# Scoring attention B in pairs of heads, and moving attention A's transposes between two projections

## The chip, the core and the metric

The kernel runs on one core of a Trainium2 chip. A core has a matrix engine (TensorE, "PE" in the profile, with its weight loads shown apart as "PEld"), a vector engine (VectorE, "DVE"), a scalar engine (ScalarE, "ACT"), GpSimd ("POOL") and SyncE ("SP"), which issues most transfers. Matrix results land in PSUM and are copied from there to SBUF by DVE or ACT. The metric is the device time of one execution in microseconds (us), of which the median of several runs is taken.

## The reference

One layer of a streaming encoder, batch 1, 256 frames of width 2048, all in float32. The change touches only the middle block, which mixes two attentions:

```python
def hybrid_mixer(u, w_in, ...):
    proj = u @ w_in
    qa, ka, va, q_lat, kv_lat, gates = jnp.split(proj, list(IN_SPLITS), axis=-1)
    y_a = chunked_relbias_attention(qa, ka, va, rel_bias) @ w_o_a   # 16 heads of 64
    y_b = mla_attention(q_lat, kv_lat, ...) @ w_o_b                 # 16 heads of 128 + 64
    g_a, g_b = jnp.split(sigmoid(gates + gate_bias), 2, axis=-1)
    return (g_a * y_a + g_b * y_b) @ w_out
```

Attention A: scores of one head are `q k^T / 8 + bias`, with q and k 64 wide. Attention B: q and k of a head consist of 128 "nope" columns of its own and 64 rotary columns; the rotary key is shared by all heads. Its scores are therefore a sum of two products, `(q_nope k_nope^T + q_rope k_rope^T) / sqrt(192)`. In both, 256 queries look at keys in chunks of 64, causally by chunk, so that the first 128 queries need 128 keys and the second 128 need 256. Then softmax, and the product with v.

Around it stand two feed-forward blocks, a cross attention to 256 memory rows, and layer norms; they are most of the work and are not touched.

## The kernel before, in words

**Precision.** Large products are made from split operands: each weight and each activation is held as hi + lo, and three products (hi hi, hi lo, lo hi) are summed. ACT makes hi (L211), DVE makes lo (L214) from the raw weights, which SP loads two items ahead. The products inside the two attentions (scores, transposes, PV) use plain f32 operands; the profile shows each such matmul as two passes, and a transpose as one.

**The list of items.** `mixer` appends items to `self.items`: a function and the weights that it needs. `run` goes through the list in order and issues the instructions. The framework's planner then fixes, at build time, the order on each engine: earlier items come first, shifted by `prio` (`NEAR` for a softmax), but where an instruction's operands aren't ready by the planner's own estimate, it takes other work that is. So the order in the trace can differ from the list.

**Attention A** works on 8 pairs of heads. `a_proj(i)` makes q and k of pair i, 128 rows for two heads of 64 (`mm_wide`, L263 and L264, two weights, each with 32 matmuls). `a_scores(i)` makes the scores of the two heads: head 0 has its q and k on rows 0 to 63 of the array, head 1 on rows 64 to 127 (L824, "64*128" in the profile). DVE adds the bias (L840; POOL loads it per head) and the softmax follows on DVE and ACT (L695 to L702). `a_trans(i)` transposes the probabilities on TensorE (L707, three 128x128 blocks a head), ACT copies them to SBUF (L713), and `a_out(i)` multiplies with v (`pv`, L854 and L855; "128*64", since a head's v has 64 columns, and the two heads lie on two column halves). Before the change, round i runs: both projections of pair i + 1, transposes of pair i - 1, scores of pair i, PV of pair i - 1.

**Attention B** works on 16 heads, one at a time. `b_proj(h)` makes q and k (24 matmuls, L252; every fourth head also v for four heads, L283). `b_scores(h)` makes, for each of two query blocks `(c0, tt, nk)` of `CAUSAL`, the 128-row product of the nope part and right behind it the 64-row product of the rotary part, into one PSUM tile:

```python
for c0, tt, nk in spans_q:
    for j, (q, k) in enumerate(parts):          # parts: (nope q, k), (rotary q, k)
        nc.tensor.matmul(ps[:, c0:c0 + nk], q[:, tt * P:(tt + 1) * P], k[:, :nk], ...)   # L824
```

The rotary queries of heads 2p and 2p + 1 lie in `self.rt[:, p, :]` on rows 0 to 63 and 64 to 127, and `self.krope` holds the rotary key on both halves. DVE adds the mask (L935), softmax, transposes (L707), copy (L713), PV (L854, L855 with 128 columns) and a split of the result into hi and lo (L242, L243). Round h runs: scores(h), transposes(h - 1), projection(h + 2), PV(h - 1).

**Buffers** that the order hangs on: four PSUM banks for scores, transposes and PV (`at_tile`), four for projections (`mm_tile`); six `w1` tiles (256 wide: q and k) and five `w2` tiles (512 wide: bias, scores, transposed probabilities).

Of the kernel before, what the change touches and what calls it, by code (L numbers as in the profile page):

```python
# [13 lines left out]
ALU = mybir.AluOpType  # L14
# [3 lines left out]
P = 128  # L18
# [9 lines left out]
A_HEADS, A_DIM = 16, 64  # L28
B_HEADS, NOPE, ROPE, V_DIM = 16, 128, 64, 128
# [9 lines left out]
SOON, NEAR, LATE = 400, 100, -400  # L39
# [44 lines left out]
class Kernel:  # L84
# [632 lines left out]
    def mixer(self, xT, st, steps):  # L717
        nc, t = self.nc, self.t
        SPANS = ((0, P), (P, 3 * P))
# [23 lines left out]
        ps = {}  # L743
# [3 lines left out]
        a, b, c = steps(1)  # L747
# [16 lines left out]
        def rms(which):  # L764
            def fn():
                if which == 0:
                    self.sq = self.block("X3")
                    self.c = self.act(["X0", "X1"])
                l = self.lat[:, 4 * which:4 * which + 4, :]
                sq = self.sq[:, 4 * which:4 * which + 4, :]  # L770
                nc.scalar.activation(sq, l, AF.Square)
                ps = self.at_tile()
                for j in range(4):
                    nc.tensor.matmul(ps[:, :S], self.ones, sq[:, j, :], start=(j == 0), stop=(j == 3))
                v, y, a = self.w1(), self.w1(), self.w1()
                nc.vector.tensor_scalar(v, ps[:, :S], 1.0 / LORA, RMS_EPS, ALU.mult, ALU.add)
                self.rsqrt(v, y, a)
                for j in range(4):
                    nc.vector.scalar_tensor_tensor(
                        l[:, j, :], l[:, j, :], self.vec(("q_a_norm", "kv_a_norm")[which], j), y,  # L780
                        ALU.mult, ALU.mult)
                self.split(l, self.c.blk(0, 4 * which, 4), self.c.blk(1, 4 * which, 4))
            self.add(fn)
# [25 lines left out]
        def a_proj(i):  # L809
            def one(k):  # L810
                def fn(w):
                    ps = self.mm_tile()
                    self.mm_wide(ps, w, xT())
                    qk[i, k] = self.total(ps)
                return fn
            for k in range(2):
                self.add(one(k), t["w_qk"][i, k])

        def scores(parts, spans_q):

            ps = self.at_tile()
            for c0, tt, nk in spans_q:
                for j, (q, k) in enumerate(parts):
                    nc.tensor.matmul(ps[:, c0:c0 + nk], q[:, tt * P:(tt + 1) * P], k[:, :nk],  # L824
                                     start=(j == 0), stop=(j == len(parts) - 1))
            return ps

        CAUSAL = ((0, 0, P), (P, 1, S))

        def a_scores(i):  # L830
            def fn():
                for j in range(2):
                    bias = self.w2((P, 3 * P))
                    nc.gpsimd.dma_start(bias, t["bias"][2 * i + j])
                    self.mask_out(bias)
                    rows = slice(64 * j, 64 * j + 64)
                    ps = scores([(qk[i, 0][rows], qk[i, 1][rows])], CAUSAL)
                    s = self.w2()
                    with self.prio(NEAR):
                        nc.vector.scalar_tensor_tensor(s[:, :3 * P], ps[:, :3 * P], 1.0 / math.sqrt(A_DIM), bias,  # L840
                                                       ALU.mult, ALU.add)
                        self.softmax(s, SPANS)
                    sc[i, j] = s
            self.add(fn)

        def a_trans(i):
            def fn():
                for j in range(2):
                    pt[i, j] = self.transpose_p(sc.pop((i, j)), (0, P, 2 * P))
            self.add(fn)  # L850

        def pv(ps, v, pT):

            nc.tensor.matmul(ps[:, :S], v(0), pT[:, :S], start=True, stop=False)  # L854
            nc.tensor.matmul(ps[:, P:S], v(1), pT[:, S:S + P], start=False, stop=True)  # L855

        def a_out(i):
            def fn():
                if i == 0:
                    oA["t"] = self.act(["H4", "H5"])  # L860
                ps = self.at_tile()
                for j in range(2):
                    c = (2 * i + j) * A_DIM
                    pv(ps[64 * j:64 * j + 64], lambda kt: va["t"][:, kt, c:c + A_DIM], pt.pop((i, j)))
                self.split(ps[:, :S], oA["t"].at(0, i), oA["t"].at(1, i))
            self.add(fn)


        rope_items = []
# [16 lines left out]
                nc.vector.tensor_tensor(self.rt[:, j, :], self.rt[:, j, :], sw[:, j, :], ALU.add)  # L886
        rope_items.append((rope_q, (), 0, LATE))

        rms(0)
        a_proj(0)  # L890
        rms(1)
        NA = A_HEADS // 2
        for i in range(NA + 1):
            if i + 1 < NA:
                a_proj(i + 1)
            if i == 1:
                self.items += rope_items
            if i > 0:
                a_trans(i - 1)
            if i < NA:  # L900
                a_scores(i)
            if i > 0:
                a_out(i - 1)

        bq, bsc, bpt, bv, oB = {}, {}, {}, {}, {}

        def b_proj(h):
            def vfn(w, g=h // 4):
                if g == 0:
                    bv["t"] = self.block("X3", (P, 2, 2, 512))  # L910
                for tt in range(2):
                    ps = self.mm_tile()
                    self.mm_tok(ps, tt, w, self.c, range(4, 8), True, True)
                    (nc.scalar.copy if tt else nc.vector.tensor_copy)(bv["t"][:, g % 2, tt, :], ps)
            if h % 4 == 0:
                self.add(vfn, t["w_v"][h // 4])

            def fn(w):
                for k in range(2):
                    ps = self.mm_tile()  # L920
                    self.mm_feat(ps[:, :S], w, [(0, k * 512 + j * P) for j in range(4)], self.c,
                                 range(4 * k, 4 * k + 4))
                    v = self.w1()
                    (nc.scalar.copy if k == 0 else nc.vector.tensor_copy)(v, ps[:, :S])
                    bq[h, k] = v
            self.add(fn, t["w_nope"][h])

        def b_scores(h):
            def fn():
                rows = slice(64 * (h % 2), 64 * (h % 2) + 64)  # L930
                ps = scores([(bq.pop((h, 0)), bq.pop((h, 1))),
                             (self.rt[rows, h // 2, :], self.krope[rows])], CAUSAL)
                s = self.w2()
                with self.prio(NEAR):
                    nc.vector.scalar_tensor_tensor(s[:, :3 * P], ps[:, :3 * P], float((NOPE + ROPE) ** -0.5),  # L935
                                                   self.mask, ALU.mult, ALU.add)
                    self.softmax(s, SPANS)
                bsc[h] = s
            self.add(fn)

        def b_trans(h):
            def fn():
                bpt[h] = self.transpose_p(bsc.pop(h), (0, P, 2 * P))
            self.add(fn)

        def b_out(h):
            def fn():
                if h == 0:
                    oB["t"] = self.act(["H0", "H1", "H2", "H3"])
                ps = self.at_tile()  # L950
                pv(ps, lambda kt: bv["t"][:, h // 4 % 2, kt, h % 4 * P:h % 4 * P + P], bpt.pop(h))
                self.split(ps[:, :S], oB["t"].at(0, h), oB["t"].at(1, h))
            self.add(fn)

        b_proj(0)
        b_proj(1)
        for h in range(B_HEADS + 1):
            if h < B_HEADS:
                b_scores(h)
            if h > 0:  # L960
                b_trans(h - 1)
            if h + 2 < B_HEADS:
                b_proj(h + 2)
            if h > 0:
                b_out(h - 1)


        mix, gt = {}, {}
# [317 lines left out]
```

## Time and profile before

| | before |
|---|---|
| time, median of 3 runs | 2561.37 us (2556.62 to 2562.75) |
| span of the profiled execution | 2560.8 us (the page gives no other time for it) |
| TensorE busy | 2544.3 us, 99% |
| TensorE weight loads busy | 2144.3 us, 84% |
| DVE busy | 1734.4 us, 68% |
| ACT busy | 1247.1 us, 49% |
| granted TensorE clock | 0.998 |
| DMA | 189 GB/s over the span |
| mixer's attentions, 832.9 to 1060.0 us | 227.1 us, TensorE busy 226.13 |

A row of the timeline gives the start in us, the length in us, the engine, the line of the kernel, the operation, the output and input tiles, the shape and how many instructions are merged; in brackets stands idle time of the engine before it and who ended it. For a matmul the shape begins with the part of the array that is used ("64*128": 64 rows, 128 columns), then the operand moved through it. "at" is a tile of the four banks for scores, transposes and PV, "mm" one of the projections' banks. A row of the windows gives, for a stretch of time, the busy us of each engine with its instruction count, the granted clock, the DMA share and GB/s.

### The profile page before, as it was taken

The numbers are of one execution on the slowest core, as the hardware profiler recorded it, in microseconds if no ns is written. First come the engines' busy times: TensorE is split into PE (matmuls) and PEld (weight loads), VectorE is DVE, ScalarE is ACT, GpSimd is POOL, SyncE is SP. The second block draws the span as 40 slices with busy tenths as digits, with TensorE's granted clock in tenths as the row PEclk, the third lists the DMA queues.
The fourth block names the chain that finished last, engine by engine and source line by source line (L and its number), as shares of the span: only waits on it lengthen the run. The fifth ranks groups of instructions, "written<-read, shape, count | busy, mean of one in ns | idle before, by whom it ended". The sixth has DMA issues, their size and how long they took to land.

```text
span 2560.8 us, 31968 instructions
## 1 busy us (share of the span) xinstructions
PE 2544.3 (99%) x12656; PEld 2144.3 (84%) x12656; DVE 1734.4 (68%) x2311; ACT 1247.1 (49%) x1678; POOL 29.7 (1%) x87
## 2 busy tenths in 40 slices
PE   9999999999999999999999999999999999999998
PEld 7888888889888888888888888888888888888886
DVE  6787547775676766555557785555888775577656
ACT  5555434554454555544444564454545553455442
POOL 0000000000000000000000000000000000000000
PEclk9999999999999999999999999999999999999999
DMA  7645554556744643345556565544554555555663
GB/s 252 240 179 207 196 197 166 214 180 204 254 168 170 199 140 114 137 178 189 192 186 255 185 218 191 195 164 136 214 190 170 214 196 196 181 197 197 215 206 138
DMA packets 74038, 488.04 MB, mean 191 GB/s; under 512 B 8608, under 2 KB 8864, under 8 KB 20768
## 3 DMA queue, kind: packets, MB, share of 16 engines
q1 hardware_dynamic: 69216, 468.18, 51.6%
q0 software_dynamic: 3808, 15.73, 2.0%
q8 instruction: 99, 1.62, 0.3%
q10 hardware_dynamic: 864, 2.10, 0.2%
q14 instruction: 51, 0.42, 0.0%
HBM read 482.69 MB, written 2.10 MB: 189 GB/s over the span
## 4 chain that ended last, share of the span: by engine, by line
PE 96%; DVE 2%; DMA 1%; ACT 0%; issue 0%; DVEq 0%; ACTq 0%
PE mm L283 31%; PE mm L263 17%; PE mm L294 14%; PE at L294 12%; PE mm L264 8%; PE mm L335 3%; PE at L335 3%; PE mm L252 2%; PE at L824 1%; DMA raw<-ffn_w_in 1%; PE at L707 1%; PE at L854 1%; DVE lo L214 0%; PE at L1124 0%; PE at L1102 0%; PE mm L624 0%
## 5 line engine op out<-in xcount | busy, mean ns | idle before, releaser
L214 DVE TENSOR_TENSOR lo<-raw,hi 128x1024 fp32r<-128x1024 f32 (+1 forms) x778 | 934.4, 1208 | 679.9 <-ACT hi L211 664.6
L211 ACT CAST hi<-raw 128x1024 fp32r<-128x1024 f32 (+1 forms) x778 | 805.6, 1040 | 951.3 <-PE mm L283 370.1
L283 PE MATMUL mm<-hi,H 128*128 128x512 f32 x1640 | 507.8, 389 | 0.0
L263 PE MATMUL mm<-T,hi 128*128 128x512 f32 x1168 | 415.1, 399 | 0.0
L283 PEld LDWEIGHTS mm<-hi,H 128*128 128x128 f32 x1640 | 307.9, 188 | 63.6
L294 PE MATMUL mm<-hi,T 128*128 128x512 f32 (+1 forms) x1152 | 346.7, 378 | 1.2 <-ACT hi L242 1.2
L264 PE MATMUL mm<-T,lo 128*128 128x256 f32 x1168 | 328.2, 281 | 0.0
L283 PE MATMUL mm<-lo,H 128*128 128x512 f32 x820 | 319.1, 389 | 0.0
L294 PE MATMUL at<-hi,T 128*128 128x512 f32 x960 | 300.7, 389 | 0.0
L263 PEld LDWEIGHTS mm<-T,hi 128*128 128x128 f32 x1168 | 219.4, 188 | 55.1 <-issue 1.5
L294 PEld LDWEIGHTS mm<-hi,T 128*128 128x128 f32 x1152 | 214.4, 188 | 36.9 <-ACT hi L242 2.1
L263 PE MATMUL mm<-H,hi 128*128 128x512 f32 x640 | 225.9, 397 | 0.0
L264 PEld LDWEIGHTS mm<-T,lo 128*128 128x128 f32 x1168 | 220.7, 189 | 0.1
L294 PE MATMUL mm<-lo,T 128*128 128x512 f32 (+1 forms) x576 | 217.9, 378 | 0.2 <-DVE lo L243 0.2
L294 PEld LDWEIGHTS at<-hi,T 128*128 128x128 f32 x960 | 180.2, 188 | 37.2
L294 PE MATMUL at<-lo,T 128*128 128x512 f32 x480 | 187.8, 391 | 0.0
L283 PEld LDWEIGHTS mm<-lo,H 128*128 128x128 f32 x820 | 154.0, 188 | 31.7
L264 PE MATMUL mm<-H,lo 128*128 128x256 f32 x640 | 178.9, 280 | 0.0
L263 PEld LDWEIGHTS mm<-H,hi 128*128 128x128 f32 x640 | 120.2, 188 | 29.0
L283 PE MATMUL mm<-hi,X 128*128 128x512 f32 x416 | 130.4, 391 | 0.0
L294 PEld LDWEIGHTS mm<-lo,T 128*128 128x128 f32 x576 | 108.1, 188 | 18.0 <-DVE lo L243 0.5
L264 PEld LDWEIGHTS mm<-H,lo 128*128 128x128 f32 x640 | 120.7, 189 | 0.0
(222 smaller groups left out, 2836.8 us busy)
## 6 DMA issues: line engine op xcount, KB each, us to landing
raw<-ffn_w_in SPq DMA_DIRECT2D x151, 1024.0 KB, 4.9
raw<-ffn_w_out SPq DMA_DIRECT2D x80, 1024.0 KB, 4.8
raw<-w_gate SPq DMA_DIRECT2D x32, 1024.0 KB, 4.8
raw<-w_qk SPq DMA_DIRECT2D x16, 1024.0 KB, 4.8
raw<-w_o_b SPq DMA_DIRECT2D x16, 1024.0 KB, 4.7
raw<-w_out SPq DMA_DIRECT2D x16, 1024.0 KB, 4.8
raw<-w_xk SPq DMA_DIRECT2D x16, 1024.0 KB, 4.9
raw<-w_xv SPq DMA_DIRECT2D x16, 1024.0 KB, 4.8
```

The source lines that it names most:

```text
L211: self.nc.scalar.copy(hi[:, :m], raw[:, c:c + m])
L214: self.nc.vector.tensor_tensor(lo[:, :m], raw[:, c:c + m], hi[:, :m].bitcast(F32), ALU.subtract)
L252: self.nc.tensor.matmul(ps, w[u][wi][:, c:c + P], x.at(xi, kt), start=(j == 0 and k == 0), stop=(j == n - 1 and k == 2),)
L263: self.nc.tensor.matmul(ps, hi, x.both(kt), start=(kt == 0), stop=False)
L264: self.last_mm = self.nc.tensor.matmul(ps[:, :S], lo, x.at(0, kt), start=False, stop=(kt == n - 1))
L283: self.last_mm = self.nc.tensor.matmul(ps, x.at(xi, kt)[:, tt * P:(tt + 1) * P], w[u][wi][:, c:c + 512], start=(start and j == 0 and k == ...
L294: self.last_mm = self.nc.tensor.matmul(ps[tt, g][:, :n], x.at(xi, kt)[:, tt * P:(tt + 1) * P], hi_lo[wi][:, g * n:(g + 1) * n], start=(kt ...
L335: self.last_mm = self.nc.tensor.matmul(bank, a[xi], hi_lo[wi][:, c:c + 512], start=own and first and j == 0, stop=own and last and j == 2)
L707: self.nc.tensor.transpose(ps[:, i * P:(i + 1) * P], s[:, c:c + P], self.ident)
L824: nc.tensor.matmul(ps[:, c0:c0 + nk], q[:, tt * P:(tt + 1) * P], k[:, :nk], start=(j == 0), stop=(j == len(parts) - 1))
L854: nc.tensor.matmul(ps[:, :S], v(0), pT[:, :S], start=True, stop=False)
```

## The change

Two things, both of order; no product is added or left out.

1. B's scores and transposes are made for a pair of heads p = (2p, 2p + 1). First come the four 128-row products of both heads, each head into a PSUM tile of its own, then the four 64-row rotary products, alternating between the two heads and so between the two row halves. Round p runs: scores(p), transposes(p - 1), projection(2p + 3), PV of both heads of p - 1, projection(2p + 4).
2. In A the transposes of pair i - 1 stand between the two projections of pair i + 1 and no longer behind both. In the last round the first projections of B take the place of A's, and the last transposes and the last PV of A stand between B's projections and first scores.

```diff
+        def b_scores(p):
             def fn():
...
+                pair = (2 * p, 2 * p + 1)
+                ps = [self.at_tile() for _ in pair]
+                for a, h in zip(ps, pair):
+                    q, k = bq.pop((h, 0)), bq.pop((h, 1))
+                    for c0, tt, nk in CAUSAL:
+                        nc.tensor.matmul(a[:, c0:c0 + nk], q[:, tt * P:(tt + 1) * P], k[:, :nk],
+                                         start=(tt == 0), stop=False, skip_group_check=True)
+                for c0, tt, nk in CAUSAL:
+                    for a, rows in zip(ps, (slice(0, 64), slice(64, P))):
+                        nc.tensor.matmul(a[:, c0:c0 + nk], self.rt[rows, p, tt * P:(tt + 1) * P],
+                                         self.krope[rows, :nk], start=False, stop=(tt == 1), skip_group_check=True)
+                for a, h in zip(ps, pair):
+                    s = self.w2()
+                    with self.prio(NEAR):
+                        nc.vector.scalar_tensor_tensor(s[:, :3 * P], a[:, :3 * P], float((NOPE + ROPE) ** -0.5),
+                                                       self.mask, ALU.mult, ALU.add)
+                        self.softmax(s, SPANS)
+                    bsc[h] = s
...
+        def b_trans(p):
             def fn():
-                bpt[h] = self.transpose_p(bsc.pop(h), (0, P, 2 * P))
+                for h in (2 * p, 2 * p + 1):
+                    bpt[h] = self.transpose_p(bsc.pop(h), (0, P, 2 * P))
...
-        for i in range(NA + 1):
-            if i + 1 < NA:
-                a_proj(i + 1)
-            if i == 1:
-                self.items += rope_items
-            if i > 0:
-                a_trans(i - 1)
-            if i < NA:
-                a_scores(i)
-            if i > 0:
-                a_out(i - 1)
+        for i in range(NA):
+            nxt = self.collect(a_proj, i + 1) if i + 1 < NA else self.collect(b_proj, 0) + self.collect(b_proj, 1)
+            cut = 1 if i + 1 < NA else 2
+            self.items += nxt[:cut]
+            if i > 0:
+                a_trans(i - 1)
+            self.items += nxt[cut:]
+            if i == 1:
+                self.items += rope_items
+            a_scores(i)
+            if i > 0:
+                a_out(i - 1)
+        b_proj(2)
+        a_trans(NA - 1)
...
-        b_proj(0)
-        b_proj(1)
-        for h in range(B_HEADS + 1):
-            if h < B_HEADS:
-                b_scores(h)
-            if h > 0:
-                b_trans(h - 1)
-            if h + 2 < B_HEADS:
-                b_proj(h + 2)
-            if h > 0:
-                b_out(h - 1)
+        NB = B_HEADS // 2
+        for p in range(NB + 1):
+            if p < NB:
+                b_scores(p)
+            if p > 0:
+                b_trans(p - 1)
+            else:
+                a_out(NA - 1)
+            if 2 * p + 3 < B_HEADS:
+                b_proj(2 * p + 3)
+            if p > 0:
+                b_out(2 * p - 2)
+                b_out(2 * p - 1)
+            if 2 * p + 4 < B_HEADS:
+                b_proj(2 * p + 4)
```

More of the change, by code (lines that the diff above doesn't have):

```diff
@@ L887, in mixer @@
         rope_items.append((rope_q, (), 0, LATE))
[L889 to L892, printed above, removed]
-        for i in range(NA + 1):
-            if i + 1 < NA:
-                a_proj(i + 1)
-            if i == 1:
-                self.items += rope_items
-            if i > 0:
-                a_trans(i - 1)
-            if i < NA:
-                a_scores(i)
-            if i > 0:
-                a_out(i - 1)
         bq, bsc, bpt, bv, oB = {}, {}, {}, {}, {}
@@ L926, in b_proj @@
             self.add(fn, t["w_nope"][h])
-        def b_scores(h):
+        def b_scores(p):
             def fn():
[L930 to L938, printed above, removed]
+                pair = (2 * p, 2 * p + 1)
[16 more added lines that the diff above has]
+                    bsc[h] = s
             self.add(fn)
-        def b_trans(h):
+        def b_trans(p):
             def fn():
-                bpt[h] = self.transpose_p(bsc.pop(h), (0, P, 2 * P))
+                for h in (2 * p, 2 * p + 1):
+                    bpt[h] = self.transpose_p(bsc.pop(h), (0, P, 2 * P))
             self.add(fn)
@@ L953, in b_out @@
             self.add(fn)
-        b_proj(0)
-        b_proj(1)
-        for h in range(B_HEADS + 1):
-            if h < B_HEADS:
-                b_scores(h)
-            if h > 0:
-                b_trans(h - 1)
-            if h + 2 < B_HEADS:
-                b_proj(h + 2)
-            if h > 0:
-                b_out(h - 1)
+        rms(0)
+        a_proj(0)
+        rms(1)
+        NA = A_HEADS // 2
+        for i in range(NA):
[27 more added lines that the diff above has]
+                b_proj(2 * p + 4)
         mix, gt = {}, {}
```

## The prediction

> **What bounds the kernel now.** I read the page from its top: engines, then the chain that ended last.
>
> ```profile
> span 2560.8 us, 31968 instructions
> PE 2544.3 (99%) x12656; PEld 2144.3 (84%) x12656; DVE 1734.4 (68%) x2311; ACT 1247.1 (49%) x1678; POOL 29.7 (1%) x87
> PE 96%; DVE 2%; DMA 1%; ACT 0%; issue 0%; DVEq 0%; ACTq 0%
> ```
>
> TensorE is busy 99% of the span and makes up 96% of the chain: a us saved on it is a us of the kernel as long as its operands come in time. Busy time says nothing about waste inside, since a matmul's bar contains its filling and draining. So I read the timeline of TensorE and take as the price of a matmul the distance from its start to the next start. First one head of attention B, alone. "x2" marks the two passes that an f32 matmul shows; "64*128" is the part of the array used, rows by columns.
>
> ```profile
> 977.21 0.60 PE L854 MATMUL at<-w,X 128*128 128x256 f32 x2
> 977.65 0.38 PE L855 MATMUL at<-w,X 128*128 128x128 f32 x2
> 977.87 0.39 PE L824 MATMUL at<-w,w 128*128 128x128 f32 x2
> 978.18 0.48 PE L824 MATMUL at<-krope,X 64*128 64x128 f32 x2
> 978.60 0.70 PE L824 MATMUL at<-w,w 128*128 128x256 f32 x2
> 979.23 0.70 PE L824 MATMUL at<-krope,X 64*128 64x256 f32 x2
> 979.86 0.55 PE L707 MATMUL at<-ident,w 128*128 128x128 f32 x3
> 980.16 0.48 PE L252 MATMUL mm<-X,hi 128*128 128x256 f32 x2
> ```
>
> With 128 rows before and behind, a 256-wide matmul takes 0.44 us (977.21 to 977.65) and a 128-wide one 0.22 (977.65 to 977.87). The 128-wide one that is followed by 64 rows takes 0.31 (977.87 to 978.18): leaving a shape costs 0.09. Between two changes it takes 0.42 (978.18 to 978.60), so entering costs another 0.11; 256 wide, 0.63 instead of 0.44. A change of shape costs TensorE 0.20 us in all. One head's scores, 977.87 to 979.86, are 1.99 us: 1.32 of work (two of 0.22, two of 0.44) and 0.67 of changes.
>
> Then attention A, whose heads already lie on the two row halves (first the pair without PV behind it, then a usual one):
>
> ```profile
> 833.11 0.93 PE L824 MATMUL at<-w,w 64*128 64x128 f32 x8
> 833.97 0.50 PE L263 MATMUL mm<-T,hi 128*128 128x512 f32 x1
> ...
> 871.32 0.82 PE L707 MATMUL at<-ident,w 128*128 128x128 f32 x6
> 872.07 0.93 PE L824 MATMUL at<-w,w 64*128 64x128 f32 x8
> 873.15 0.81 PE L854 MATMUL at<-w,H 128*64 128x256 f32 x3 [0.15 <-ACT w L713]
> ...
> 874.33 0.50 PE L263 MATMUL mm<-T,hi 128*128 128x512 f32 x1
> ...
> 885.73 0.82 PE L707 MATMUL at<-ident,w 128*128 128x128 f32 x6
> ```
>
> Eight passes (two heads, 128 and 256 wide) take 0.86 us, 833.11 to 833.97, both changes included. Serial they would be 1.32 + 0.20 = 1.52: the two halves do run side by side. Behind the usual pair PV waits for the copy of the transposed probabilities (L713).
>
> **The change, part by part, each cost from these rows.**
>
> *B's scores by pairs.* No matmul is added or removed; their order changes. Per pair before: 2 x 1.99 = 3.98. After: four 128-row matmuls, 0.22 + 0.44 + 0.22 + 0.44 = 1.32, plus leaving 0.09; then eight 64-row passes in the order and shape of A's, 0.86. Sum 2.27, saved 1.71 (0.66 by overlap, 1.05 by changes). Eight pairs: **13.7 us**. The heads write two different score tiles, as A's do. From below, if the halves did not overlap, the block would be 1.52: saved 1.05 a pair, 8.4. From above, nothing is below A's row.
>
> Here a rule speaks against the row. The Trainium skill, page "TensorE: Matmul & The Clock Gate", Part 3, The mechanism, says that matmuls start and end strictly in program order. By it a head's second pass would hold back the other head's first, and only neighbouring passes would overlap: 0.11 + 0.11 + 0.21 + 0.21 + 0.21 of passes and 0.20 of changes are 1.05 instead of 0.86, 1.5 us more over eight pairs. The eight passes in 0.86 speak against it for A; for B no run shows it yet, so it is a rival below.
>
> *What pairing holds longer.* Scores take two score banks of four at once; the transposes behind them need the banks of the PV before, evacuated during a projection and 2.27 us of scores. Six w1 buffers hold q and k of exactly three heads; the next projection's copies come behind the scores that free them. I cost both at nothing; the cover is the projection behind the transposes, 2.95 us (from 980.16 to the end of the round at 983.11, next row). If it were gone, PV or a projection would wait for the evacuation of a bank or a buffer on DVE, and the next scores, queued behind it on TensorE, with it; that is rival (c). The first projections of B are now written ahead of the last pair of A; they cost the same there.
>
> ```profile
> core 0: us, PE busy (x) PEld busy (x) DVE busy (x) ACT busy (x) POOL busy (x), PEclk, DMA share, GB/s
> 977.21:983.11 5.89, 5.89 (x41) 4.93 (x40) 3.87 (x12) 3.04 (x8) 0.00 (x0) 1.00 0.30 89
> ```
>
> A head's round lasts 5.89; DVE works 3.87 of it, ACT 3.04. A pair's round becomes 2 x 5.89 - 1.71 = 10.07, with DVE at 7.74 and ACT at 6.08: 77% and 60%, close enough to name, not a bound. Transposes of a pair come a whole round behind its scores, so its two softmaxes have some 8 us.
>
> *A's transposes between the two projections.* Before, a usual pair costs 871.32 to 874.33 = 3.01: six transposes 0.66 and leaving 0.09, scores 0.86, the wait, PV. After: transposes 0.66 among matmuls of their own shape, leaving from the projection 0.09, scores 0.86, then PV without the wait. What PV costs when both heads' copies are there stands in the last A pair:
>
> ```profile
> 942.10 0.48 PE L824 MATMUL at<-w,w 64*128 64x128 f32 x2
> 942.51 0.44 PE L707 MATMUL at<-ident,w 128*128 128x128 f32 x2
> 942.88 0.93 PE L824 MATMUL at<-w,w 64*128 64x256 f32 x6
> 943.74 0.66 PE L854 MATMUL at<-w,H 128*64 128x256 f32 x4
> 944.54 0.38 PE L252 MATMUL mm<-X,hi 128*128 128x256 f32 x1
> ...
> 952.95 0.65 PE L854 MATMUL at<-w,H 128*64 128x256 f32 x2
> ...
> 954.26 0.49 PE L824 MATMUL at<-w,w 128*128 128x128 f32 x2
> ...
> 955.09 0.65 PE L854 MATMUL at<-w,H 128*64 128x256 f32 x2
> ...
> 955.89 0.70 PE L824 MATMUL at<-w,w 128*128 128x256 f32 x2
> ```
>
> 943.74 to 944.54 = 0.80, both heads side by side on the column halves. Sum 0.66 + 0.09 + 0.86 + 0.80 = 2.41, saved 0.60, on six usual pairs 3.6. Against it: the transposes now come one projection earlier, and the softmax may be late. Its last steps for the pair scored at 872.07:
>
> ```profile
> 879.61 0.55 DVE L840 SCALAR_TENSOR_TENSOR w<-at,w 128x384 f32<-128x384 f32 x1
> ...
> 882.85 0.54 DVE L702 TENSOR_SCALAR w<-w,sm_r 128x128 f32<-128x128 f32 x2
> ```
>
> It ends at 883.39. The first projection ends halfway between 874.33 and 885.73, at 880.03: 3.36 us too early, if nothing else moved. Two things move. The second head's work starts only at 879.61 because its bias tile takes a buffer that the transposes free; with transposes earlier, that load (POOL's queue, one per head, as before) is issued a projection earlier, before the scores instead of behind. And the planner fills a wait: in the rows above it slipped two late transposes into the middle of the scores (942.51) and moved whole projections of B ahead of them. So I expect late transposes to fall inside the second projection. Bounds: 0 and 3.36 a pair; nearest is filling, at about 0.1 a pair: 0.6. Net **3.0 us**. The weights' loads on SP's queue keep their order.
>
> *Where A meets B.* Pair 7's scores were cut up: 942.10 to 943.74 = 1.64, less two transposes at 0.11, against 0.86: 0.56. Its PV came in two pieces, 952.95 to 954.26 and 955.09 to 955.89, together 2.11 less two transposes 0.22, against 0.80: 1.09. The new order puts a projection between these steps, but the softmax of pair 7 may again come late: between 0 and 1.65, I take half, **0.8 us**.
>
> *Sum.* 13.7 + 3.0 + 0.8 = 17.5 on a span of 2560.8: 2543.3. The page gives no other time for this execution; the median of the three runs, 2561.37, lies 0.6 above its span, and the same is added here: **2543.9 us**. The runs themselves go from 2556.62 to 2562.75.
>
> **The rivals.**
> (a) *The halves overlap less than A's.* For it: B's 64-row matmuls add to tiles that the 128-row ones began, A's do not. Against: A's rows otherwise match in shape and order. In strict order +1.5, 2545.4; without overlap 8 x 0.66 = +5.3, 2549.2. Chance 0.08.
> (b) *The change doesn't keep its order:* the planner slips late transposes or PV into a pair's scores, as at 942.51, and each adds two changes, 0.4. Against: in the steady rounds of B (977.21 to 980.16) nothing was slipped in. If half the pairs lose their gain, 7 us back: 2551. Chance 0.10.
> (c) *DVE sets the pace of B.* For it: two softmaxes at once, 77%, and queues that wait in order. Against: 2.3 us free a round. If B's rounds stay at 2 x 5.89, only A's part is left: 2561.4 - 3.8 = 2557.6; half of it, 2550.7. Chance 0.07. The Trainium skill, page "TensorEngine Tiling (Array Packing)", PSUM Bottleneck, warns of it: packing speeds up TensorE, not the copies out of PSUM, which may then bind. The 3.87 of 5.89 is against it here.
> (d) *Slower: TensorE waits for A's softmax.* If the transposes are queued right behind the projection and the softmax keeps its 883.39, each of the eight pairs waits 3.36 (the last stands behind a single projection too), and with it the second projection, queued behind on TensorE, and ACT's next weight conversion, which waits for that projection's buffers: 26.9, so 2543.9 + 26.9 = 2570.8. It eats the gain from 17.5 / 8 = 2.2 a pair on. For it: the softmax did end 3.36 behind that point. Against: the filling above, and the earlier bias. Chance 0.05.
>
> **How the numbers follow.** Forecast 0.70, with its own range 2540 to 2549 (A from 0 to 3.6, the seam 0 to 1.65, spread of the runs). 0.3%, 7.7 us, is about what a measurement can tell from no change: the line is 2553.7. Faster: forecast, (a), nearly all of (b), half of (c): 0.90. Same: the rest of (c), some of (b) and (d): 0.06. Slower: 0.04, nearly all of (d). The range is 2538 to 2552: below, all bounds at their best (13.7 + 3.6 + 1.65 = 19.0 saved, 2542.4) and 4 us for the runs, whose lowest lay 4.75 under their median; above, (a) and (b). It leaves out about 0.12, most of (c) and (d).
>
> **What would show it.** In TensorE's timeline in B, per pair: eight passes of "at<-w,w" with 128 rows in 1.41, then eight of "at<-krope,X" within 0.86, 2.27 from the first score to the first transpose, a round of 10.1, and no steps of 0.42 and 0.63. In A: transposes (L707) between the projection's matmuls, PV (L854) 0.86 behind the first score, no wait for L713, and PV in 0.80. It would be wrong if TensorE shows idle time before L707, if transposes stand between score rows, or if the krope passes start one behind another.

## The result and the profile after

The changed kernel takes 2537.52 us (median of 4 runs, 2537.06 to 2538.35); the kernel before, timed beside it, takes 2558.99 us (4 runs, 2556.01 to 2562.75). The ratio is 0.9919, 95% interval 0.9904 to 0.9933. By medians 21.5 us are gone, between the two profiled executions 25.6 (spans 2560.8 and 2535.2). The forecast was a saving of 17.5 us, to 2543.9 us. The runs of before lie in groups, near 2555, near 2557 and at 2561 to 2563 us; the profiled execution, on which the forecast's sum stands, is of the last group.

First the top of the page after and the first line of its chain of waits:

```profile
span 2535.2 us, 31980 instructions
PE 2520.8 (99%) x12656; PEld 2136.5 (84%) x12656; DVE 1730.9 (68%) x2311; ACT 1246.2 (49%) x1678; POOL 29.7 (1%) x87
PE 99%; DVE 1%; DMA 0%; issue 0%; DVEq 0%; ACT 0%; ACTq 0%
```

TensorE has the same 12656 matmuls and is busy 23.5 us less: nearly all that was gained lies inside its bars. Next, TensorE's timeline of after over a pair of heads in B (L919 is now the line of the 128-row scores, L923 that of the rotary ones):

```profile
971.44 0.28 PE L252 MATMUL mm<-X,lo 128*128 128x256 f32 x1
971.56 1.48 PE L919 MATMUL at<-w,w 128*128 128x128 f32 x8
972.97 0.93 PE L923 MATMUL at<-krope,X 64*128 64x128 f32 x8
973.82 0.88 PE L707 MATMUL at<-ident,w 128*128 128x128 f32 x6
974.45 0.48 PE L252 MATMUL mm<-X,hi 128*128 128x256 f32 x2
```

From the first score to the first transpose, 971.56 to 973.82, it is 2.26 us, against 2 x 1.99 before. The 128-row block takes 1.41, the rotary block 0.85. By the starts of the single passes in the trace, the second head's pass follows the first's by 6 to 7 ns. The windows give the whole round of that pair, with the engines in the order PE, PEld, DVE, ACT, POOL:

```profile
971.56:981.59 10.03, 10.03 (x69) 8.71 (x68) 7.31 (x20) 5.51 (x15) 0.00 (x0) 1.00 0.37 112
```

Then a round of A in TensorE's timeline of after: transposes, scores and PV, and the start of the next scores.

```profile
871.75 0.93 PE L824 MATMUL at<-w,w 64*128 64x128 f32 x8
872.62 0.66 PE L854 MATMUL at<-w,H 128*64 128x256 f32 x4
...
879.06 0.28 PE L264 MATMUL mm<-T,lo 128*128 128x256 f32 x1
879.18 0.81 PE L707 MATMUL at<-ident,w 128*128 128x128 f32 x6
879.75 0.47 PE L263 MATMUL mm<-T,hi 128*128 128x512 f32 x1
...
885.47 0.93 PE L824 MATMUL at<-w,w 64*128 64x128 f32 x8
```

The transposes stand among the projection's matmuls, and PV begins 0.87 behind the first score. The round is 13.72 us (871.75 to 885.47), where it was 14.41. What TensorE waited for in the attentions (total us, times, longest) was L713's copy in before and is L702's softmax in after; first the row of before, then that of after:

```profile
PE at L854 <- ACT w L713: 0.9, 6, 0.2
```

```profile
PE at L707 <- DVE w L702: 0.4, 2, 0.3
```

**Where the 25.6 us came from.** I set the two traces side by side by matmul: the k-th from the end in one against the k-th from the end in the other. Up to the end of the attentions after is ahead by 18.5 us. The rest is not in the code that was changed. 5.9 us come in the gate stage, some 1050 to 1370 us, which multiplies with the gates' weights and the two output weights and was not touched. The windows of the projections' line L263 alone, first in before, then in after:

```profile
1059.50:1371.50 312.00, 311.95 (x883) 165.93 (x883) 1.00 0.54 193
```

```profile
1040.50:1347.00 306.50, 306.50 (x885) 165.34 (x885) 1.00 0.55 196
```

The bracket counts L263's matmuls, each of which is followed by one of L264: 312.00 / 883 = 353.3 ns a pair of them before, 306.50 / 885 = 346.3 after (by the starts in the trace 353.3 and 346.7). The granted clock is 1.00 in both, and nothing waits. Over 884 pairs that is 5.8 us. Last, some 1.4 us belong to one wait in a feed-forward block of before's profiled execution, in its timeline:

```profile
1905.43 1.67 PE L335 MATMUL mm<-X,X 128*128 128x512 f32 x6 [0.78 <-DVE H L243]
```

It is missing in another execution of the same kernel (e0_before_again below), so it is no part of the change. Between the two stages 0.2 us are lost again.

### The profile page after: what moved, and what is told of

It is laid out like the page before. It is cut to its first block, busy times and chain, and to the rows that moved or that the text cites. A ratio compares the mean times of both kernels' runs of the same rounds, so it can differ in the third digit from the quotient of the medians.

```text
span 2535.2 us, 31980 instructions
## 1 busy us (share of the span) xinstructions
PE 2520.8 (99%) x12656; PEld 2136.5 (84%) x12656; DVE 1730.9 (68%) x2311; ACT 1246.2 (49%) x1678; POOL 29.7 (1%) x87
## 4 chain that ended last, share of the span: by engine, by line
PE 99%; DVE 1%; DMA 0%; issue 0%; DVEq 0%; ACT 0%; ACTq 0%
PE mm L283 33%; PE mm L263 16%; PE mm L294 15%; PE at L294 13%; PE mm L264 8%; PE mm L335 3%; PE at L335 3%; PE mm L252 2%; PE at L707 1%; PE at L1141 0%; PE at L1119 0%; PE at L854 0%; PE at L386 0%; PE at L919 0%; PE mm L624 0%; PE at L624 0%
## 5 line engine op out<-in xcount | busy, mean ns | idle before, releaser
L263 PE MATMUL mm<-T,hi 128*128 128x512 f32 x1168 | 412.2, 396 | 0.0
L264 PE MATMUL mm<-T,lo 128*128 128x256 f32 x1168 | 327.9, 281 | 0.0
L263 PEld LDWEIGHTS mm<-T,hi 128*128 128x128 f32 x1168 | 219.1, 188 | 51.4 <-issue 1.0
L263 PE MATMUL mm<-H,hi 128*128 128x512 f32 x640 | 223.5, 393 | 0.0
L264 PEld LDWEIGHTS mm<-T,lo 128*128 128x128 f32 x1168 | 220.7, 189 | 0.1
L264 PE MATMUL mm<-H,lo 128*128 128x256 f32 x640 | 178.8, 279 | 0.0
L263 PEld LDWEIGHTS mm<-H,hi 128*128 128x128 f32 x640 | 119.8, 187 | 26.9
L264 PEld LDWEIGHTS mm<-H,lo 128*128 128x128 f32 x640 | 120.8, 189 | 0.0
```

What stands on the lines that cost most here:

```text
L263: self.nc.tensor.matmul(ps, hi, x.both(kt), start=(kt == 0), stop=False)
L264: self.last_mm = self.nc.tensor.matmul(ps[:, :S], lo, x.at(0, kt), start=False, stop=(kt == n - 1))
```

## The experiments

**The two parts alone.** e0_before_again is the kernel before once more. e1_pairs_only takes B's pairs and leaves A's order; e2_a_only takes A's order and leaves B's heads single:

```diff
 # e1_pairs_only, against after
-        for i in range(NA):
...
-            self.items += nxt[:cut]
-            if i > 0:
-                a_trans(i - 1)
-            self.items += nxt[cut:]
+        for i in range(NA + 1):
+            if i + 1 < NA:
+                a_proj(i + 1)
...
+            if i > 0:
+                a_trans(i - 1)
 # e2_a_only, against after
-                pair = (2 * p, 2 * p + 1)
...
+                ps = scores([(bq.pop((h, 0)), bq.pop((h, 1))),
+                             (self.rt[rows, h // 2, :], self.krope[rows])], CAUSAL)
...
-        b_proj(2)
```

> The kernel before, unchanged. Its four runs so far lie in two groups (2562.75 and 2561.37; 2556.62 and 2556.01), 6 us apart. In its profile a pair of projection matmuls (512 and 256 wide) in the gate stage takes 353.3 ns, in the profile after 346.7 ns: 884 pairs, 5.9 us. Theory H (history): the matmul stream of the gate stage falls into one of a few rhythms and keeps it; runs of one and the same kernel fall into either, so its runs again lie in two groups about 6 us apart, near 2556 and 2562, and a profile with a span near 2555 shows 346.7 ns, one near 2561 shows 353.3. Rival P (program): the rhythm belongs to the built program (addresses, order); then every profile of this kernel shows 353.3 ns, whatever its time, and the two groups come from a wait elsewhere.

> Only attention B by pairs; attention A and the seam in the order of before. Theory T (the terms add up): scores of a pair 2.27 us from the first score to the first transpose, as after (2.26), A's usual rounds 14.4 us as before, and 13.7 to 15 us less than before from the first A score to the gate stage; in all 2545 if the gate rhythm is 353.3 ns, 2540 if it is 346.7. Rival S (the parts need each other): without A's new order the pairs wait for banks or buffers, idle time stands in front of scores or PV, and less than 10 us are saved. On the rhythm: if ending B with pairs made the gate stage fast, it is 346.7 here.

> Only attention A's new order (transposes between the projections, the seam without the earlier third projection); attention B head by head as before. Theory T: A's usual rounds fall from 14.41 us to between 13.72 and 14.17 as after, B's head stays at 1.99 us from the first score to the first transpose, and 3 to 5 us are saved before the gate stage; in all 2556 with a gate rhythm of 353.3 ns, 2550 with 346.7. Rival S: the gain of A in the profile after came from B's pairs behind it, and the rounds stay at 14.4. On the rhythm: if B's pairs made the gate stage fast, it is 353.3 here.

| | median us | runs (range) | ratio to before | 95% | ahead of before at B's end | gate stage, ns a pair |
|---|---|---|---|---|---|---|
| e0_before_again | 2557.37 | 11 (2554.73 to 2563.26) | 1.0008 | 0.9998 to 1.0018 | 0.1 | 353.3 |
| e1_pairs_only | 2541.51 | 5 (2541.32 to 2542.15) | 0.9944 | 0.9932 to 0.9957 | 14.0 | 346.7 |
| e2_a_only | 2556.44 | 11 (2550.31 to 2557.74) | 0.9995 | 0.9986 to 1.0004 | 4.4 | 353.3 |

The sixth column is worked out from the traces, matmul by matmul, against before's. 14.0 + 4.4 = 18.4 against 18.5 for both. But 0.3 of e1's and 0.4 of e2's lead stand ahead of A's first scores, where neither changes anything; counted from those scores it is 13.7 + 4.0 = 17.7 against 18.5. So the parts add to within 0.8 us, and most of the 0.8 lies in A's rounds, of which the five from the scores of pair 1 to those of pair 6 take 70.0 us in e2_a_only and 69.4 in after. By their times alone one would say that A's order is worth nothing. Its trace is ahead when B ends, but ten of its eleven runs lie at 2556 to 2558; the profiled one has its gate stage at 353.3. The one other run is at 2550.31, 6 us lower.

**Is the overlap of the halves there?** e3_one_half lets both heads take their rotary operands from rows 0 to 63, so that they no longer lie on two halves; the second head's rotary part is then that of the first.

```diff
-                    for a, rows in zip(ps, (slice(0, 64), slice(64, P))):
+                    for a, rows in zip(ps, (slice(0, 64), slice(0, 64))):
```

> The kernel after, but the rotary scores of both heads of a pair are taken from rows 0 to 63 (the second head gets the first head's rotary query: this part of the result is changed, the work and its order are not). Theory O (the halves overlap): the eight 64-row passes of a pair take 1.52 us and not 0.86, from the first score to the first transpose 2.92 and not 2.26, +0.66 a pair, +5.3 us in all: 2543 at the same gate rhythm. Rival L (the block is short because weights are loaded ahead once the shape stays, not because two halves work at once): the block stays at 0.86 to 1.0 and the time within 1 us of the kernel after.

2543.44 us (5 runs, 2541.17 to 2543.88), ratio 0.9948 (0.9935 to 0.9962). TensorE's timeline of e3_one_half:

```profile
974.34 1.57 PE L923 MATMUL at<-krope,X 64*128 64x128 f32 x8
975.85 0.87 PE L707 MATMUL at<-ident,w 128*128 128x128 f32 x6
```

The block takes 1.51 us instead of 0.85, 0.66 more. At the end of B the kernel is 13.2 us ahead of before, 5.25 less than after: that is what the overlap is worth.

**Are the changes of shape worth the rest?** e5_by_head keeps the pairs but makes each head's 128-row products and then its own rotary ones: four changes a pair instead of two, and no overlap.

```diff
-                for a, h in zip(ps, pair):
+                for a, h, rows in zip(ps, pair, (slice(0, 64), slice(64, P))):
...
-                for c0, tt, nk in CAUSAL:
-                    for a, rows in zip(ps, (slice(0, 64), slice(64, P))):
+                    for c0, tt, nk in CAUSAL:
```

> The kernel after, but within a pair each head first makes its two 128-row products and then its two rotary ones: no two row halves side by side, and four changes of shape a pair instead of two. By the prices of before (0.20 a change, work 1.32 a head) a head takes 0.22 + 0.44 + 0.09 + 0.11 + 0.22 + 0.44 + 0.09 = 1.61 us, plus 0.11 to enter the next head: 3.33 from the first score to the first transpose of a pair instead of 2.26 (before: 3.98). Theory T (the gain is changes of shape plus overlap, separately): +1.07 a pair, +8.6 us, 2546 at a gate rhythm of 346.7 ns. Rival O (nearly all of the gain is the overlap, changes are hidden once weights are loaded ahead): 2.92 a pair as with one row half, +5.3, 2543.

2544.81 us (4 runs, 2544.64 to 2545.60), ratio 0.9956 (0.9941 to 0.9971). TensorE's timeline of e5_by_head:

```profile
974.38 0.82 PE L919 MATMUL at<-w,w 128*128 128x128 f32 x4
975.12 0.92 PE L922 MATMUL at<-krope,X 64*128 64x128 f32 x4
975.97 0.92 PE L919 MATMUL at<-w,w 128*128 128x128 f32 x4
976.83 0.92 PE L922 MATMUL at<-krope,X 64*128 64x128 f32 x4
977.68 0.88 PE L707 MATMUL at<-ident,w 128*128 128x128 f32 x6
```

974.38 to 977.68 is 3.30 us a pair against 2.26: 1.04 more, of which e3 gives 0.66 to the overlap and 0.38 stay for two changes, 0.19 each. Over eight pairs the blocks give 8 x 1.04 = 8.3 us. At its end the kernel is 8.5 us behind after by matmul, at the same rhythm in its gate stage; that the two figures are so close is partly chance, since this execution is 0.4 us ahead at A's first scores and then loses 1.1 us in A's rounds, where TensorE waits up to 0.9 us for a softmax (L702).

**How late may A's transposes be put?** e6_trans_first writes them ahead of both projections, where the softmax can't be done.

```diff
-            cut = 1 if i + 1 < NA else 2
+            cut = 0
```

> The kernel after, but A's transposes stand in the list ahead of both projections of the next round, right behind the PV before. Theory F (the planner fills): they are slipped in where the planner believes the softmax to be ready, which is 18 to 22 matmuls into the first projection for the first head and some 10 matmuls later for the second; TensorE waits there at most 0.5 us a pair, as it does in two rounds of the kernel after, and the time stays within 2 us of it, 2538 to 2540. Rival W (the planner's belief is early, and TensorE stands in front of the transposes until the softmax ends, as in the prediction's slower rival): 1 to 3 us of idle time a pair in front of the transposes, 8 to 20 us in all, 2546 or more.

2538.47 us (4 runs, 2538.37 to 2540.21), ratio 0.9932 (0.9917 to 0.9947), about 1 us behind after. TensorE's timeline of e6_trans_first shows where the transposes went:

```profile
873.33 0.40 PE L855 MATMUL at<-w,H 128*64 128x128 f32 x4
877.49 0.30 PE L707 MATMUL at<-ident,w 128*128 128x128 f32 x1 [0.16 <-DVE w L702]
877.75 0.38 PE L707 MATMUL at<-ident,w 128*128 128x128 f32 x2
879.59 0.27 PE L707 MATMUL at<-ident,w 128*128 128x128 f32 x1
879.82 0.38 PE L707 MATMUL at<-ident,w 128*128 128x128 f32 x2
886.14 0.93 PE L824 MATMUL at<-w,w 64*128 64x128 f32 x8
```

They are written ahead of the projection that begins behind 873.33 and were issued at 877.49 and 879.59, in the middle of it, with a wait of 0.16 us. The order written in the list is not the order that TensorE gets: the planner fills in other work until it believes the softmax done.

**What is the rhythm of the gate stage?** Here I tried to change it without touching what it computes. e4_interrupts is after with one unread matmul ahead of 12 of the 16 gate columns (a column is 56 pairs), of three kinds in turn; e7_nudge is after with an unread 128-row matmul ahead of three other stages (at 756, 1442 and 1622 us), of which only the first, ahead of the latent projections, lies before the gates, and 280 us before them.

```diff
 # e4_interrupts
+                    if k == 0 and m % 4:
+                        d = self.at_tile()
+                        if m % 4 == 1:      # 128 rows, f32
+                            nc.tensor.matmul(d[:, :S], self.ones, self.krope, start=True, stop=True)
+                        elif m % 4 == 2:    # 64 rows, f32
+                            nc.tensor.matmul(d[:, :S], self.ones[0:64], self.krope[0:64], start=True, stop=True)
+                        else:
+                            nc.tensor.transpose(d[:, :P], self.ident, self.ident)
 # e7_nudge, in each of the three stages
+                    nc.tensor.matmul(self.at_tile()[:, :P], self.ones, self.ones, start=True, stop=True)
```

> The kernel after, with one extra matmul, whose result nobody reads, in front of 12 of the 16 gate columns: for columns 1, 5, 9, 13 an f32 matmul with 128 rows, for 2, 6, 10, 14 one with 64 rows, for 3, 7, 11, 15 a transpose, for 0, 4, 8, 12 nothing. By their prices (0.44, 0.44 + 0.20, 0.11) they cost 4 x 1.19 = 4.8 us. Between two of them lie 56 pairs of projection matmuls. Theory H (the rhythm is set by the last interruption and kept until the next): the 56 pairs behind an interruption change their rhythm by its kind, as before A's projections (353 ns a pair behind a change of shape, 346.7 behind the f32 matmuls of the norm), and columns without one keep that of the column before; with 353 ns behind the 64-row ones the time is 2537.5 + 4.8 + 1.5 = 2544. Rival P (the rhythm belongs to the built program): all columns stay at 346.7 ns, time 2542.

> The kernel after, with one extra f32 matmul of 128 columns (0.22 us, result unread) in front of each of three stages whose pairs of projection matmuls run at 353.2 ns in every profile so far: the latent projections (144 pairs), the keys of the memory (128) and the first queries of the cross attention (64 a head). Theory H (an interruption draws the rhythm anew, 346.7 or 353.3 ns, whatever its kind): each of the stages has about an even chance to fall to 346.7, worth 0.95, 0.85 and 0.4 us; the time lies between 2536 and 2538.2. Rival P (these stages are slow because of their own operands): all three stay at 353.2 and the time rises by 0.7, to 2538.1.

e4_interrupts: 2545.03 us (6 runs, 2544.57 to 2550.53), ratio 0.9963 (0.9950 to 0.9975). Worked out from the starts in its trace, ns a pair by column, the interrupted pair left out:

```
column   0      1      2      3      4      5      6      7      8      9      10     11     12     13     14     15
ahead    none   128    64     transp none   128    64     transp none   128    64     transp none   128    64     transp
ns       346.8  353.4  346.7  346.7  346.7  353.3  346.7  353.3  353.3  346.8  353.1  353.3  353.3  353.3  346.7  346.7
```

Both values stand in one execution, and a column without an interruption keeps the one before it. The kind of matmul does not decide: 128 rows was followed by 353 three times and by 347 once, 64 rows by 347 three times and by 353 once, a transpose by each twice. The time is near theory H's 2544, but a rhythm set by the kind of matmul did not come, and rival P's single rhythm did not either.

e7_nudge: 2544.42 us (6 runs, 2543.65 to 2546.89), ratio 0.9949 (0.9937 to 0.9962), 6.9 us behind after. The windows of L263 in its gate stage:

```profile
1040.50:1353.50 313.00, 313.00 (x887) 166.43 (x887) 1.00 0.54 193
```

313.00 / 887 = 352.9: the order of after can run at the longer rhythm too, and then 6.1 of the 7.4 us between the two profiled executions lie in the gate stage. The rest is 1.0 us ahead of the gates, in the latent stage and the attentions, and 0.3 behind. The three stages right behind the unread matmuls stayed at 353 ns, as rival P had it, while the gate stage, which the edit leaves alone, changed; neither expectation had that. All six runs of e7_nudge lie at 2543.65 us or more and all four of after at 2538.35 or less, so the difference goes with the edit; by what way is not shown. In any case the pairs in B do not fix the rhythm.

**Is before's lower group the shorter rhythm?** e8_before_look and e9_before_look are the kernel before, profiled twice more to catch an execution near 2555 us.

> The kernel before, unchanged, for a profile of one of its faster executions. Theory H: a span near 2553.5 goes with 346.7 ns a pair in the gate stage (5.9 us less there than at 353.3 ns), a span near 2560 with 353.3. Rival: the gate stage is at 353.3 ns in both, and the 6 us lie elsewhere.

> The same again, a second execution of the kernel before, with the same two expectations: span near 2553.5 with 346.7 ns a pair in the gate stage, or near 2560 with 353.3 (history); 353.3 ns in either (program).

They came at 2561.64 and 2561.74 us, one run each. The windows of L263 in e8_before_look:

```profile
1059.50:1371.50 312.00, 312.00 (x884) 165.92 (x883) 1.00 0.53 193
```

Again 353 ns; e9 is the same by its starts. No profile caught the lower group, so no trace answers the question. The 6 us between the groups fit the rhythm, and the times say more: of the 54 runs of before that were timed beside the experiments, 35 lie at 2554.35 to 2556.16 us (median 2555.2), 16 at 2560.8 to 2563.0 and three between. The lower group is 17.7 us above after's 2537.5 and 13.7 above e1_pairs_only's 2541.5, which is what the traces give for these changes by matmul at one rhythm. This is an argument and not a proof.

**Both kernels at one rhythm.** The last two put the same unread 64-row matmul ahead of each of the 16 gate columns, in before (e10_before_cut) and in after (e11_after_cut).

```diff
+                    if k == 0:
+                        d = self.at_tile()
+                        nc.tensor.matmul(d[:, :S], self.ones[0:64], self.krope[0:64], start=True, stop=True)
```

> Before, with one unread 64-row matmul (two passes) ahead of each of the 16 gate columns; its result goes nowhere. Asked: is the quick rhythm of the gate stage (346.7 ns a pair of projection matmuls) open to the kernel before too, or does the new order of the attentions bring it? Such a matmul, 256 columns wide between two changes of shape, takes 0.63 us, so 16 of them cost some 10.1 us. Theory D (the rhythm is drawn anew at every interruption, whatever ran before): some of the 16 columns run at 346.7 ns and others at 353.3, and the profiled execution comes to 2561 + 10.1 less 0.37 us for each quick column: 2566 to 2571. Rival K (the quick rhythm belongs to the pairs of heads in B): all columns at 353.3, 2571.

> After, with the same 16 unread matmuls ahead of the gate columns. Theory D: some columns at 346.7 ns and others at 353.3, some 2537.5 + 10.1 = 2547.6 plus 0.37 for each slow column: 2548 to 2553. Rival K: all columns at 346.7, 2547.6. Against the kernel before with the same matmuls, theory D leaves a difference of 17.8 give or take 3 (no rhythm favours either), rival K one of about 23.

e10_before_cut: 2573.85 us (4 runs, 2571.12 to 2574.49), ratio 1.0057 (1.0038 to 1.0077). e11_after_cut: 2553.64 us (10 runs, 2552.52 to 2555.97), ratio 0.9986 (0.9977 to 0.9996). Both forms of the expectation missed: by the starts, the first column runs at 346.7 ns a pair and the other 15 at 353.3, in both kernels alike. From TensorE's timeline of e10_before_cut, two starts in the first column that are 42 pairs apart, 14.56 us or 346.7 ns a pair:

```profile
1060.80 0.40 PE L263 MATMUL mm<-T,hi 128*128 128x512 f32 x1
...
1075.36 0.40 PE L263 MATMUL mm<-H,hi 128*128 128x512 f32 x1
```

This kernel has no pairs of heads in B, so rival K, that the shorter rhythm belongs to them, is refuted. An interruption also cost more than the 0.63 us put on it: 20.60 us from one column's start to the next, less 56 x 0.3533, is 0.8. From its own start to the next it does take 0.63; the rest falls on the pairs on either side. The windows of L263 over the 15 columns, e10_before_cut and then e11_after_cut:

```profile
1076.40:1384.60 308.20, 298.79 (x840) 157.81 (x840) 1.00 0.53 189
```

```profile
1058.10:1366.30 308.20, 298.81 (x840) 157.81 (x840) 1.00 0.53 189
```

Windows of the same length hold the same 840 pairs in either. So the two kernels can be compared with no difference of rhythm in the gate stage. By matmul after is 18.3 us ahead when B ends and 18.0 at the end of the span (2572.2 and 2554.2). **The change itself is worth 18 us**; what the first pair of profiles showed beyond that is rhythm and one wait. By their medians the two are 20.2 us apart: the profiled execution of e11_after_cut is the slowest of its ten runs, and what makes the others up to 3.5 us shorter is not shown.

## Why the prediction was right, and where it was not

- *B's pairs, 13.7 us.* Right. 2.26 against 2.27 from the first score to the first transpose, a round of 10.03 against 10.07, eight pairs x (3.98 - 2.26) = 13.8; e1_pairs_only gains 13.7 from A's first scores to B's end. Both parts are shown apart: overlap 5.25 (0.66 x 8 were put on it), and of the six changes that pairing saves in each pair e5_by_head takes back two: 8.3 - 5.25 = 3.1 (2 x 0.20 x 8 = 3.2).
- *Rival (a), less overlap or strict order.* Refuted. The rule of the Trainium skill, page "TensorE: Matmul & The Clock Gate", Part 3, The mechanism, as the prediction read it, would have made the rotary block 1.05; it is 0.85, with the two halves' passes starting 6 to 7 ns apart. For f32 matmuls of two passes the rule does not hold in the sense in which the prediction weighed it; the trace shows when the passes start and not in which order they stand in the program, so it does not show that the rule itself is broken.
- *Costs of a change of shape.* The prediction's 0.20 is 0.19 in e5_by_head. The Trainium skill, page "TensorEngine Tiling (Array Packing)", Key Properties, says that changing the tiling mode drains TensorE; the trace fits that and adds the price, in later starts at each change, but does not show the drain itself.
- *A's rounds, 3.0 us.* Right in sum, and in part by luck. From the scores of pair 1 to those of pair 6, before takes 72.08 us and after 69.44; round 0 loses 0.33, which the prediction did not have, and for the round of pair 6, which in the two orders holds different projections, I count 0.7, an estimate from an undisturbed round (14.41 less 13.72): 72.08 - 69.44 - 0.33 + 0.7 = 3.0. An undisturbed round saves that 0.69 and not the 0.60 put on it; three of the rounds in after last longer than 13.72 (13.92, 14.17, 13.91) because the softmax ends behind the first projection, together 0.84, where 0.6 were put. These misses cancel. The longest of the three, in TensorE's timeline of after, where the second head's transposes come late:

```profile
906.81 0.49 PE L707 MATMUL at<-ident,w 128*128 128x128 f32 x3
907.46 0.30 PE L707 MATMUL at<-ident,w 128*128 128x128 f32 x1 [0.16 <-DVE w L702]
```

- *Rival (d), TensorE waits for A's softmax.* Refuted, even with the transposes written a projection earlier still. TensorE's wait in e6_trans_first is 0.3 us at most, not 3.36 each time (the longest in any profile here is the one of 0.9 in e5_by_head):

```profile
PE at L707 <- DVE w L702: 0.8, 4, 0.3
```

  The planner's filling was the right argument.
- *Rival (c), DVE.* Refuted: 7.31 of 10.03 us (7.74 were put), and TensorE has no idle time in the round.
- *Rival (b) and the seam, 0.8 us.* The size was off. 18.3 - 13.8 - 3.0 leave 1.5 (as sharp as the 0.7 above) for the place where A meets B, near the bound of 1.65 and not half of it. In TensorE's timeline of after:

```profile
946.51 0.30 PE L707 MATMUL at<-ident,w 128*128 128x128 f32 x1 [0.27 <-DVE w L702]
946.77 0.38 PE L707 MATMUL at<-ident,w 128*128 128x128 f32 x2
...
948.01 0.39 PE L919 MATMUL at<-w,w 128*128 128x128 f32 x2
948.23 0.38 PE L707 MATMUL at<-ident,w 128*128 128x128 f32 x2
948.45 1.25 PE L919 MATMUL at<-w,w 128*128 128x256 f32 x6
949.63 0.93 PE L923 MATMUL at<-krope,X 64*128 64x128 f32 x8
950.49 0.66 PE L854 MATMUL at<-w,H 128*64 128x256 f32 x4
```

  What rival (b) feared happened, but only here: two late transposes slipped in behind B's first 128-row product, in one pair of eight. Transposes between score rows were one of the prediction's own signs of being wrong. It cost no change of shape, since a transpose uses the same 128 rows; (b) had priced a slip at two changes. And PV is uncut, which is what the half had allowed for.
- *What failed:* the step from the sum to the time, which took the other 2543 us of the one execution as fixed. They were not. The prediction lies 6.4 us above the median (2543.9 against 2537.5): 5.9 from the gate stage and 1.4 from the wait at L335, neither of them the change, 0.8 because the change gave 18.3 and not 17.5, less 1.2 because that execution's time was not 0.6 above its span (executions for which both are known lie 1.8 above, as 2560.95 and 2559.1 in e0_before_again; so it was the run at 2562.75), and less 0.5 by which the median lies above after's own profiled run, 2537.06. The mis-sized term is the spread of the runs: 4 us were added below for it, and it was taken as noise of either kernel alike. The time ends 0.5 us below the range. Had the sum stood on before's lower group, 2555.2 us, the same 17.5 would have given 2537.7. In the profiles without unread matmuls the gate stage ran at the shorter rhythm in every kernel with B's pairs and at the longer one in every kernel without them.

Why stays open: e7_nudge and e11_after_cut show that the longer rhythm is open to the new order too, and the first column of e10_before_cut that the shorter one is open to the old order.

## What to carry to other kernels

Where matmuls of less than the full rows alternate with full ones, group them: a change of shape cost about 0.2 us here, and two halves from different heads side by side took 0.85 us instead of 1.51. Read the price of a matmul from start to start in a place of the same shape in the same trace; that gave the score blocks of B to within 0.02 us and an undisturbed round of A to within 0.1. And compare traces by matmul, stage by stage, before a difference in the total is credited to an edit: e2_a_only saved 4 us by matmul and timed as no change, and after gained 6 us in a stage that nobody touched.

## What the runs showed of the hardware that was not expected

A long row of projection matmuls, 512 wide and 256 wide in turn, runs at 353.3 or 346.7 ns a pair at a granted clock of 1.00 and with no wait, and keeps its value for hundreds of pairs (884 in before and in after). Unread matmuls in between can change it (e4_interrupts), and so did an edit whose only unread matmul ahead of the stage lies 280 us before it (e7_nudge). Both values occur in both orders of the heads (e10_before_cut, e11_after_cut), and the kind of matmul does not decide it. Over the gate stage it is worth 6 us, 0.23% of this kernel, close to the 0.3% that a measurement can tell from no change. What sets it is not shown.
